# A decoder layer's gated FFN input projection as seven half-size products

## The chip, the cores and the metric

The kernel runs on one core of a Trainium2 chip. The metric is the device time of one launch, in microseconds, as the median of several runs. The profile is one further execution, taken with the hardware profiler; its span runs from the first instruction to the last.

## The reference, cut to what matters

One layer of a decoder: 512 tokens, 2048 features, float32 throughout. Two token mixers (a gated linear recurrence and a forgetting attention) are merged by gates, projected, normalised and added to the residual stream. Then comes a SwiGLU feed-forward part with 5632 inner features. Only its first product, 512 x 2048 by 2048 x 11264, is computed differently after the change.

```python
def rms_norm(x, w):
    y = x * lax.rsqrt(jnp.mean(x * x, axis=-1, keepdims=True) + RMS_EPS)
    return y * w

x = x + rms_norm(merged @ w_o, norm_mix_post)
h = rms_norm(x, norm_ffn_pre)
gate, up = jnp.split(h @ w_ffn_in, 2, axis=-1)     # D_FF = 5632 columns each
x = x + rms_norm((jax.nn.silu(gate) * up) @ w_ffn_down, norm_ffn_post)
```

## The kernel before, in words

TensorE (PE) multiplies in a float32 format whose operands are rounded (fp32r). Every float32 operand is therefore split into a high and a low part, and one product is three accumulating matmuls (`mm3`, L151 to L155, with the weights stationary; `mm3t`, L157 to L161, with the activations stationary).

All weights pass as one list `seq` of pieces of 128 x 1024 values. `make_w` (L125) loads a piece into one of three raw buffers on SP's queue, copies it to fp32r on ACT (`wh`, L137) and subtracts on DVE to get the rest (`wl`, L138). There are five buffers each of `wh` and `wl` (`NHALF`). `next_w` (L144) makes the wanted piece and the two that follow it in the list (`AHEAD` is 3) and hands out the wanted one.

The order of the work on each engine is not the order of the program text. A planner runs through the traced program with its own costs and places each instruction, earlier ones in the text first, as soon as its operands and a free buffer are there; what comes out is a fixed order for each engine and each queue. `tc.issue_after` and `tc.keep_in_program_order` add edges to it.

The stages: projections of the first norm's output and the mixers; gates and merge; the output projection w_o; FFN in; FFN down. `rows_product` computes w_o and FFN down in token rows, with eight banks of PSUM (four token tiles by two blocks of 512 columns) for each half of the 2048 columns. Of the second half the last four row tiles (`TAIL`) run token tile by token tile, so the four pieces of weights that they use stay in their buffers up to the end.

`wo_done` (L678 to L693) takes each block of the output projection: on DVE the product with the norm's gain, on ACT the square with its row sum, and, after the fourth block of a token tile, on POOL the power -0.5, on DVE four updates of the residual (L690), and their stores to DRAM (L691). After the second token tile `take_x1(0)` (L697) turns the first 256 tokens: PE transposes (L704), ACT multiplies by the gain of the next norm and rounds (L712), DVE forms the rest (L713). The other 256 tokens follow while the first two column pairs of FFN in are computed for 256 tokens at a time (tile f). The 1/rms of the token is taken from squares on ACT (L747) and multiplies the results afterwards, as a row along tokens (`r2b`).

The other 42 column pairs are two products of 48 matmuls each (tiles fg and fu): 128 weight columns stationary, 512 tokens moving. `swiglu` (L720) reads them from PSUM, on DVE with `r2b` (L723, L725), on ACT the sigmoid, on DVE two products more. Of the 44 results ten are stored in DRAM and read back for FFN down; the others stay in SBUF. `act_split` (L778) splits a result into its two parts for each half of FFN down.

Tiles of 128 x 512 values share two pools, 43 buffers named big and 32 named x.

Of the kernel before, what the change touches and what calls it, by code (L numbers as in the profile page):

```python
# [8 lines left out]
F32 = mybir.dt.float32  # L9
F32R = mybir.dt.float32r  # L10
# [17 lines left out]
NBIG = 43  # L28
# [3 lines left out]
AHEAD = 3  # L32
XAHEAD = 2
GATE_AHEAD = 5
NSPILL = 10
TAIL = 4
X1_AT = 6
# [3 lines left out]
def block_kernel(ctx: ExitStack, tc: tile.TileContext, x, w_in, b_fox_f, hgrn_lb_logits, hgrn_norm_w,  # L41
# [16 lines left out]

    psum = {}
# [18 lines left out]
    seq = []  # L78

    def cols(w, c0, kt):  # L80
        """one column tile of 128, as pieces of 8 row tiles"""
# [34 lines left out]
    korder = [(k + NSPILL) % KF for k in range(KF)]  # L116
    for half in range(2):
        for k in korder:
# [32 lines left out]
    def mm3(ps, wh, wl, xh, xl, first, last):  # L151
        """one accumulating float32 product in float32r parts: w lo x hi + w hi x lo + w hi x hi"""
# [4 lines left out]
    def mm3t(ps, wh, wl, xh, xl, first, last):  # L157
        """the same with x stationary"""
# [4 lines left out]
    def proj(name, xs, n_k, kind="acc"):  # L163
        """[128 columns, tokens] of the next weight columns"""
# [8 lines left out]
    def split(src, name, kind="big"):  # L173
        """float32 -> two float32r parts whose sum it is"""
# [16 lines left out]
    def rsqrt_mean(dst, ssq, n):  # L191
        """dst = (ssq / n + eps) ** -0.5"""
# [5 lines left out]
    # x by tiles of 128 features, all tokens  # L198
# [6 lines left out]
    # per-feature vectors, one row of 128 each, then transposed  # L205
# [19 lines left out]
    # the token's 1/rms multiplies the projections afterwards  # L225
# [39 lines left out]
    def token_row(r, name):  # L265
        """[token, tile] -> the same values along tokens, on every partition"""
# [5 lines left out]
        row = big(name)  # L272
# [14 lines left out]
    # lower bounds: row 0 of the cumulated softmax over the two rows of logits  # L287
# [16 lines left out]
    chunk0 = big("chunk0", shape=(P, 256))  # L304
# [3 lines left out]
    # lmask[p, level, which, block, l]: which pairs part at a level (see hgrn_head)  # L308
    lmask = [big("lmask0", shape=(P, 4, 2, 64)), big("lmask1", shape=(P, 3, 2, 64))]
# [10 lines left out]
    # Inside a head the chunks of 128 tokens lie as 0, 2, then 1, 3 with their tokens reversed, so that one matrix  # L320
    # of 128 x 128 holds, for two chunks, the scores of all pairs that part at a level.
# [9 lines left out]
    def by_parity(fn, out, *ins):  # L331
        """fn on the even chunks, then on the odd ones, from token order into the paired one"""
# [8 lines left out]
    def hgrn_in(h, part, ps, r):  # L341
        """what a head takes from one of its four projections"""
# [26 lines left out]
    def hgrn_head(h, r):  # L369
        """the rest of a head, in steps"""  # L370
# [24 lines left out]
        # scores within a chunk of 128: the diagonal, then pairs (s, t) by the level at which they part  # L395
# [22 lines left out]
        for li, L in enumerate(LEVELS):  # L418
# [7 lines left out]
            # keys, then queries; each by pair of chunks, then position with the chunk's place in the pair at level L  # L426
# [59 lines left out]
    def step():  # L486
        """the heads under way, each a step further"""
# [45 lines left out]
    cum = big("cum", shape=(H, S))  # L533
# [12 lines left out]
    def fox_head(h, r):  # L546
        """the attention of a head, in steps"""
# [130 lines left out]
    def wo_done(t, c, ps):  # L678
# [13 lines left out]
        if t == 1:  # L692
            take_x1(0)  # L693

    x1s = []

    def take_x1(th):  # L697
        hs = slice(th * 256, (th + 1) * 256)
        for k in range(0, KD, 2):
            pt = bank(f"x1p{th}_{k}", (P, 2, 2, P))  # L700
            for kk in range(2):
                for t in range(2):
                    c, q = (k + kk) // 4, (k + kk) % 4
                    nc.tensor.transpose(out=pt[:, kk, t, :], in_=xr[2 * th + t][c][:, q * P : (q + 1) * P],  # L704
# [131 lines left out]
```

## Time and profile before

| what | value |
|---|---|
| median of 3 runs | 2919.47 us (2918.87 to 2919.93) |
| span of the profiled execution | 2918.0 us |
| the three runs above the profiled span | 0.9 to 1.9 us, the median 1.5 us |
| PE busy | 2893.9 us (99%), 13346 matmuls |
| weight loads of PE (PEld) | 2404.1 us (82%) |
| DVE busy | 1213.9 us (42%) |
| ACT busy | 893.8 us (31%) |
| POOL busy | 36.5 us (1%) |
| moved between HBM and the core | 302 MB, 104 GB/s in the mean |

The profiled execution has no launch time around its span that the page shows: its own time is the span, and the runs lie 0.9 to 1.9 us above it. Busy times of matmuls overlap, so that a busy PE can still issue faster or slower; its rate is read from the starts of neighbouring matmuls. DVE, ACT and POOL take their instructions one after the other in the planned order, and the busy times of neighbours on DVE and ACT overlap by a little.

### The profile page before, as it was taken

What the parts mean: (1) busy time and instruction counts of PE and PEld (TensorE: products, weight loads), DVE (VectorE), ACT (ScalarE), POOL (GpSimd) and SP (SyncE); (2) the same over time, 40 slices, a digit from 0 to 9 for tenths busy, and PEclk for the clock granted to TensorE, in tenths of its full rate; (3) what the DMA queues carried; (4) which work ended last, traced back from release to release, by engine and by line L of the source; (5) the groups of instructions that cost most, each with busy time, mean ns of one, the idle gap of its engine ahead of it and who ended that gap; (6) DMA issues with size and microseconds to landing.
All of it is one profiled execution on the core that took longest, in us unless ns stands there. A gap on an engine that the chain in (4) does not pass through costs nothing.

```text
span 2918.0 us, 32478 instructions
## 1 busy us (share of the span) xinstructions
PE 2893.9 (99%) x13346; PEld 2404.1 (82%) x13346; DVE 1213.9 (42%) x1747; ACT 893.8 (31%) x1165; POOL 36.5 (1%) x72
## 2 busy tenths in 40 slices
PE   9999999999999999999999999999999999999998
PEld 7788888888888888888898888888888888888887
DVE  4776665333343433342373333333333334334333
ACT  4554544222232342232252222222222223323231
POOL 0100000000000000000000000000000000000000
PEclk9999999999999999999999999999999999999999
DMA  6323233333333333352363333333333334222342
GB/s 159 102 71 86 75 87 82 99 94 102 94 88 88 88 91 94 97 170 94 109 194 106 110 103 94 101 94 96 100 94 101 94 100 145 95 96 99 108 144 95
DMA packets 438967, 302.06 MB, mean 104 GB/s; under 512 B 11241, under 2 KB 410650, under 8 KB 438818
## 3 DMA queue, kind: packets, MB, share of 16 engines
q1 hardware_dynamic: 438818, 299.98, 35.2%
q8 instruction: 105, 1.72, 0.2%
q14 instruction: 44, 0.36, 0.0%
HBM read 288.91 MB, written 11.03 MB: 103 GB/s over the span
## 4 chain that ended last, share of the span: by engine, by line
PE 98%; ACT 1%; DVE 1%; issue 0%; DMA 0%; POOL 0%; SPq 0%; DVEq 0%; POOLq 0%; ACTq 0%
PE dn L159 5%; PE dn L161 5%; PE dn L160 5%; PE fg L154 5%; PE fu L154 5%; PE fg L155 5%; PE fu L155 5%; PE fu L153 5%; PE fg L153 5%; PE b L153 3%; PE b L154 3%; PE b L155 3%; PE p L153 3%; PE p L154 3%; PE p L155 3%; PE ga L155 2%
## 5 line engine op out<-in xcount | busy, mean ns | idle before, releaser
L137 ACT ACTIVATE wh<-wr 128x1024 fp32r<-128x1024 f32 (+1 forms) x518 | 544.5, 1052 | 1566.3 <-PE fg L154 358.3
L138 DVE TENSOR_TENSOR wl<-wr,wh 128x1024 fp32r<-128x1024 f32 (+1 forms) x518 | 629.8, 1216 | 716.1 <-ACT wh L137 715.9
L153 PE MATMUL fg<-x1l,wh 128*128 128x512 f32 x672 | 261.4, 389 | 0.0
L154 PE MATMUL fg<-x1h,wh 128*128 128x512 f32 x672 | 261.4, 389 | 0.0
L155 PE MATMUL fg<-x1h,wl 128*128 128x512 f32 x672 | 261.4, 389 | 0.0
L153 PE MATMUL fu<-x1l,wh 128*128 128x512 f32 x672 | 261.4, 389 | 0.0
L154 PE MATMUL fu<-x1h,wh 128*128 128x512 f32 x672 | 261.4, 389 | 0.0
L155 PE MATMUL fu<-x1h,wl 128*128 128x512 f32 x672 | 261.4, 389 | 0.0
L153 PEld LDWEIGHTS fu<-x1l,wh 128*128 128x128 f32 x672 | 126.2, 188 | 26.2
L153 PEld LDWEIGHTS fg<-x1l,wh 128*128 128x128 f32 x672 | 126.2, 188 | 26.2
L154 PEld LDWEIGHTS fu<-x1h,wh 128*128 128x128 f32 x672 | 126.2, 188 | 26.1
L154 PEld LDWEIGHTS fg<-x1h,wh 128*128 128x128 f32 x672 | 126.2, 188 | 26.1
L155 PEld LDWEIGHTS fu<-x1h,wl 128*128 128x128 f32 x672 | 126.2, 188 | 26.1
L155 PEld LDWEIGHTS fg<-x1h,wl 128*128 128x128 f32 x672 | 126.2, 188 | 26.1
L725 DVE TENSOR_TENSOR act<-fu,r2b 128x512 f32<-128x512 f32 x42 | 29.0, 692 | 138.6 <-PE fu L155 138.6
L723 DVE TENSOR_TENSOR g<-fg,r2b 128x512 f32<-128x512 f32 x42 | 29.0, 692 | 138.3 <-PE fg L155 138.3
L153 PE MATMUL f<-x1l,wh 128*128 128x256 f32 x128 | 36.7, 288 | 0.0
L154 PE MATMUL f<-x1h,wh 128*128 128x256 f32 x128 | 36.2, 284 | 0.0
L155 PE MATMUL f<-x1h,wl 128*128 128x256 f32 x128 | 36.2, 283 | 0.0
L515 DVE TENSOR_TENSOR sga<-ya,sga 128x512 f32<-128x512 f32 x16 | 11.1, 692 | 52.8 <-PE ya L155 52.8
L508 DVE TENSOR_TENSOR sga<-ga,rb 128x512 f32<-128x512 f32 x16 | 11.1, 692 | 51.9 <-PE ga L155 51.9
L727 DVE TENSOR_TENSOR act<-act,g 128x512 f32<-128x512 f32 (+1 forms) x46 | 30.7, 668 | 1.4
(1944 smaller groups left out, 5927.7 us busy)
## 6 DMA issues: line engine op xcount, KB each, us to landing
wr<-in_w_ffn_in_dram SPq DMA_DIRECT2D x168, 512.0 KB, 3.9
wr<-in_w_in_dram SPq DMA_DIRECT2D x166, 512.0 KB, 3.9
wr<-in_w_ffn_down_dram SPq DMA_DIRECT2D x88, 512.0 KB, 3.4
wr<-in_w_o_dram SPq DMA_DIRECT2D x32, 512.0 KB, 3.2
wr<-in_w_up_a_dram SPq DMA_DIRECT2D x16, 512.0 KB, 4.1
wr<-in_w_up_b_dram SPq DMA_DIRECT2D x16, 512.0 KB, 3.9
wr<-in_w_ffn_in_dram SPq DMA_DIRECT2D x32, 256.0 KB, 3.6
wr<-in_w_in_dram SPq DMA_DIRECT2D x32, 128.0 KB, 2.2
```

The costliest lines, as they stand in the source:

```text
L137: hi = nc.scalar.activation(wh[:, 0:width], raw[:, 0:width], AF.Copy)
L138: lo = nc.vector.tensor_tensor(wl[:, 0:width], raw[:, 0:width], wh[:, 0:width].bitcast(F32), ALU.subtract)
L153: nc.tensor.matmul(ps, lhsT=wh, rhs=xl, start=first, stop=False)
L154: nc.tensor.matmul(ps, lhsT=wh, rhs=xh, start=False, stop=False)
L155: nc.tensor.matmul(ps, lhsT=wl, rhs=xh, start=False, stop=last)
L159: nc.tensor.matmul(ps, lhsT=xl, rhs=wh, start=first, stop=False)
L160: nc.tensor.matmul(ps, lhsT=xh, rhs=wl, start=False, stop=False)
L161: nc.tensor.matmul(ps, lhsT=xh, rhs=wh, start=False, stop=last)
L508: nc.vector.tensor_tensor(sg_, psg_, rb, ALU.mult)
L723: nc.vector.tensor_tensor(g, psg, r, ALU.mult)
L725: nc.vector.tensor_tensor(a, psu, r, ALU.mult)
L727: nc.vector.tensor_tensor(a, a, g, ALU.mult)
```

## The change: what it does

The projection is computed by one level of Strassen's scheme in the form with seven products. Features (8 row tiles of 128 each half, `KH`), tokens (256 each half) and the gate and up columns are the halves. With a, b, c, d for the 1024 x 128 pieces of the weights (a: first features, gate; b: first features, up; c: second features, gate; d: second features, up), the products are of h11 with a, h12 with c, s4 with d, h22 with a combination of all, and s1, s2, s3 with b - a, a + (d - b) and d - b. The combinations of weights are made in place by DVE on the raw pieces, before the split. Each product is 24 matmuls of 256 tokens.

- The input is normalised in full before the projection: after each token tile's residual update `wo_done` squares it again, takes the power, and multiplies the token rows; `r2b` is gone. `take_h` replaces `take_x1` and makes the token and feature combinations on DVE.
- Phase one computes p1 and p2 of the first five column tiles (`NJ0`) from the first 256 tokens. Phase two computes their other five products, with the four pieces loaded again as needed. The other 39 column tiles run all seven products in a row.
- The pieces of w_ffn_in no longer pass through `seq`, whose w_ffn_down pieces now follow those of w_o. They have their own functions (`raw_w`, `load_to`, `parts_to`): loads nine products ahead, splits three ahead, in the same `wh` and `wl` buffers. Pieces b and d (c too in phase one) use three raw buffers of a new pool that takes the room of six tiles moved to `headp`; `NBIG` is 37.
- All 44 results go to DRAM, and FFN down reads each of them twice, three ahead.

```diff
-    for th in range(2):
-        for k in range(0, KD, 2):
-            r = w_ffn_in[k * P : (k + 2) * P, :]
-            seq.append([((0, 512), 2, r[:, 0:256]), ((512, 1024), 2, r[:, DFF : DFF + 256])])
-    for j in range(2, KF):
-        cols(w_ffn_in, j * P, KD)
-        cols(w_ffn_in, DFF + j * P, KD)
...
             nc.sync.dma_start(x1d[t * P : (t + 1) * P, c_ * S : (c_ + 1) * S], x1)
-        if t == 1:
-            take_x1(0)
+            nc.scalar.activation(mo[t, c_], x1, AF.Square, accum_out=s2_[:, t, c_ : c_ + 1])
+        s = smallp.tile([P, 1], F32, name="wos")
+        nc.vector.tensor_reduce(s, s2_[:, t, :], AX.X, ALU.add)
+        r = smallp.tile([P, 1], F32, name="wor")
+        rsqrt_mean(r, s, D)
+        for c_ in range(4):
+            nc.vector.tensor_scalar_mul(mo[t, c_], xr[t][c_], r)
+        if t % 2 == 1:
+            take_h(t // 2)
...
+    def parts_of(src, i, names, kind):
...
+        nc.scalar.activation(hi, src, AF.Copy)
+        nc.vector.tensor_tensor(lo, src, hi.bitcast(F32), ALU.subtract)
...
+    def take_h(th):
+        for i in range(KH):
...
+            raw = big(f"hr{th}_{i}")
+            for kk in range(2):
+                k = i + kk * KH
+                nc.scalar.activation(raw[:, kk * 256 : (kk + 1) * 256],
+                                     pt[:, kk, :, :].rearrange("p t n -> p (t n)"), AF.Copy,
+                                     scale=w_fpre_f[:, k : k + 1])
+            if th == 0:
+                hraw.append(raw)
+                parts_of(raw, i, ("h11", "h12"), "x")
+                continue
+            h1 = hraw[i]
+            h11, h12, h21, h22 = h1[:, 0:256], h1[:, 256:512], raw[:, 0:256], raw[:, 256:512]
+            s32 = big(f"hs{i}")
+            nc.vector.tensor_tensor(s32[:, 0:256], h11, h21, ALU.subtract)
+            nc.vector.tensor_tensor(h21, h21, h22, ALU.add)
+            parts_of(raw, i, ("s1", "h22"), "x")
+            nc.vector.tensor_tensor(s32[:, 256:512], h21, h11, ALU.subtract)
+            nc.vector.tensor_tensor(h12, h12, s32[:, 256:512], ALU.subtract)
+            parts_of(s32, i, ("s3", "s2"), "big")
+            parts_of(h12, i, ("s4",), "big")
...
+    work = [(j, p) for j in range(NJ0) for p in ("p1", "p2")]
+    work += [(j, p) for j in range(NJ0) for p in ("p3", "p7", "p5", "p6", "p4")]
+    work += [(j, p) for j in range(NJ0, KF) for p in ("p1", "p3", "p7", "p5", "p6", "p2", "p4")]
...
+    def parts_to(i):
...
+            if p == "p7":
+                nc.vector.tensor_tensor(d, d, b, ALU.subtract)
+            elif p == "p5":
+                nc.vector.tensor_tensor(b, b, a, ALU.subtract)
+            elif p == "p6":
+                nc.vector.tensor_tensor(a, a, d, ALU.add)
+            elif p == "p4":
+                nc.vector.tensor_tensor(c, a, c, ALU.subtract)
+            src = {"p1": a, "p2": c, "p3": d, "p7": d, "p5": b, "p6": a, "p4": c}[p]
+            wh = wp.tile([P, 1024], F32R, tag="wh", name=f"fh{n}", bufs=NHALF)
+            wl = wp.tile([P, 1024], F32R, tag="wl", name=f"fl{n}", bufs=NHALF)
+            nc.scalar.activation(wh, src, AF.Copy)
+            nc.vector.tensor_tensor(wl, src, wh.bitcast(F32), ALU.subtract)
...
+    for n, (j, p) in enumerate(work):
+        load_to(n + LOAD_AHEAD)
+        parts_to(n + AHEAD)
...
+        for i in range(KH):
+            cs = slice(i * P, (i + 1) * P)
+            xh, xl = hx[i][WITH[p]]
+            mm3(ps, wh[:, cs], wl[:, cs], xh, xl, i == 0, i == KH - 1)
...
+        if p == ("p2" if j >= NJ0 else "p6"):
+            t_ = tt[j] = big(f"t{j}")
+            g1 = gt[j][:, second_half]
+            nc.vector.tensor_tensor(t_[:, first_half], prod[j, "p6"], g1, ALU.add)
+            if j >= NJ0:
+                nc.vector.tensor_tensor(gt[j][:, first_half], prod[j, "p2"], g1, ALU.add)
+            nc.vector.tensor_tensor(t_[:, second_half], prod[j, "p7"], t_[:, first_half], ALU.add)
+            nc.vector.tensor_tensor(ut[j][:, second_half], prod[j, "p5"], t_[:, second_half], ALU.add)
+            nc.vector.tensor_tensor(ut[j][:, first_half], ut[j][:, first_half], t_[:, first_half], ALU.add)
+        if p == "p4":
+            g, u, t_ = gt.pop(j), ut.pop(j), tt.pop(j)
+            nc.vector.tensor_tensor(g[:, second_half], t_[:, second_half], prod[j, "p4"], ALU.subtract)
+            nc.scalar.activation(t_, g, AF.Sigmoid)
+            nc.vector.tensor_tensor(g, g, t_, ALU.mult)
+            nc.vector.tensor_tensor(g, g, u, ALU.mult)
+            nc.sync.dma_start(actd[j * P : (j + 1) * P, :], g)
...
+    def act_load(n):
+        if n < 2 * KF and n not in act:
+            act[n] = big(f"act{n}")
+            nc.sync.dma_start(act[n], actd[n % KF * P : (n % KF + 1) * P, :])
...
-        return split(act[k], f"as{half}_{k}", kind="x")
+        for n in range(3):
+            act_load(half * KF + k + n)
+        return split(act.pop(half * KF + k), f"as{half}_{k}", kind="x")
```

Two products of 256 tokens share one bank of PSUM. For the column tiles from the sixth on they pair as p1 and p3, p7 and p5, p6 and p2, and p4 alone; the reads shown and a few copies and adds left out above take them from there.

## Rows read from the trace of the kernel before

**Rows 1.** The page's chain of waits, by engine.

```profile
PE 98%; ACT 1%; DVE 1%; issue 0%; DMA 0%; POOL 0%; SPq 0%; DVEq 0%; POOLq 0%; ACTq 0%
```

**Rows 2.** Busy time by stretch (us, engines in the header's order).

```profile
core 0: us, PE busy (x) PEld busy (x) DVE busy (x) ACT busy (x) POOL busy (x), PEclk, DMA share, GB/s
...
1464.50:1480.00 15.50, 15.37 (x127) 14.98 (x126) 14.60 (x25) 14.54 (x35) 0.54 (x1) 1.00 0.78 245
...
1600.00:2400.00 800.00, 800.00 (x3531) 662.66 (x3530) 275.77 (x295) 175.22 (x184) 0.00 (x0) 1.00 0.34 99
...
2900.00:2918.00 18.00, 10.29 (x46) 8.19 (x44) 12.15 (x23) 2.89 (x10) 1.63 (x3) 0.87 0.48 179
```

**Rows 3.** Tiles fg and fu (512 wide): ns min/median/max, first and last start.

```profile
L153 PE MATMUL fg<-x1l,wh x672: 389/389/396, 1515.8 to 2418.2; 128*128 128x512 f32 x168
...
L155 PE MATMUL fu<-x1h,wl x672: 388/389/389, 1527.1 to 2429.5; 128*128 128x512 f32 x168
```

**Rows 4.** Timeline of PE, 256 wide: start, us; first and last of 36.

```profile
1509.78 0.28 PE L154 MATMUL f<-x1h,wh 128*128 128x256 f32 x1
...
1513.98 0.28 PE L153 MATMUL f<-x1l,wh 128*128 128x256 f32 x1
```

**Rows 5.** Tile f: one of its three groups of weight loads.

```profile
L153 PEld LDWEIGHTS f<-x1l,wh x128: 186/192/192, 1464.5 to 1515.3; 128*128 128x128 f32 x128
```

**Rows 6.** Timeline of PE: the projection's first matmul, and the down product's.

```profile
1464.67 0.28 PE L153 MATMUL f<-x1l,wh 128*128 128x256 f32 x1
...
2431.27 0.50 PE L159 MATMUL dn<-wh,as_10l 128*128 128x512 f32 x1 [1.38 <-DVE as_10l L178]
```

**Rows 7.** Timeline of PE: transposes of x1, the first of four such rows.

```profile
1476.41 1.47 PE L704 MATMUL x1p<-ident,xr 128*128 128x128 f32 x12
```

**Rows 8.** Timeline of DVE: neighbours of 1024, 512 and 256 columns.

```profile
1487.50 2.35 DVE L138 TENSOR_TENSOR wl<-wr,wh 128x1024 fp32r<-128x1024 f32 x2
1489.77 0.68 DVE L268 TENSOR_TENSOR r2bd<-ident,r4b 128x512 f32<-128x512 f32 x1
1490.37 1.21 DVE L138 TENSOR_TENSOR wl<-wr,wh 128x1024 fp32r<-128x1024 f32 x1
...
1497.30 0.42 DVE L725 TENSOR_TENSOR act<-f,r2b 128x256 f32<-128x256 f32 x1
1497.64 0.41 DVE L726 TENSOR_TENSOR g<-g,g_0s 128x256 f32<-128x256 f32 x1
```

**Rows 9.** Timeline of ACT: copies of 256 (four), 1024 and 512 columns.

```profile
1483.20 1.63 ACT L712 ACTIVATE x1h<-x1p,vec 128x256 fp32r<-128x256 f32 x4
1484.86 1.06 ACT L137 ACTIVATE wh<-wr 128x1024 fp32r<-128x1024 f32 x1
1485.83 1.19 ACT L712 ACTIVATE x1h<-x1p,vec 128x256 fp32r<-128x256 f32 x3
...
2431.23 0.61 ACT L177 ACTIVATE as_12h<-act 128x512 fp32r<-128x512 f32 x1
```

**Rows 10.** Waits, 1520 to 2430 us: total, times, longest.

```profile
ACT wh L137 <- PE fg L154: 358.3, 82, 4.4
DVE wl L138 <- ACT wh L137: 320.4, 126, 4.1
```

**Rows 11.** Timeline of ACT, POOL and DVE: one token tile of the output projection.

```profile
1448.79 0.63 ACT L747 ACTIVATE mo<-xr 128x512 f32<-128x512 f32 x1
...
1451.17 0.56 POOL L196 TENSOR_TENSOR wor<-rs_v,mhalf 128x1 f32<-128x1 f32 x1 [5.20 <-DVE rs_v L195]
...
1451.77 2.74 DVE L690 SCALAR_TENSOR_TENSOR xr<-mo,wor,xr 128x512 f32<-128x512 f32 x4 [0.68 <-POOL wor L196]
```

**Rows 12.** Groups by line and shape: a product with one value per row.

```profile
L576 DVE TENSOR_SCALAR b0p<-b0p,sm 128x512 f32<-128x512 f32 x1 | 0.5, 486 | 0.0
```

**Rows 13.** DMA issues, 1520 to 2430 us: count, KB each, us to landing.

```profile
wr<-in_w_ffn_in_dram SPq DMA_DIRECT2D x160, 512.0 KB, 3.9
...
actr<-actd SPq DMA_DIRECT2D x10, 256.0 KB, 7.1
```

More of the change, by code (lines that the diff above doesn't have):

```diff
@@ L27 @@
 LEVELS = (64, 32, 16, 8, 4, 2, 1)
-NBIG = 43
+NBIG = 37
+NHEAD = 6
+NRAWX = 3
+NJ0 = 5
 NX = 32
@@ L32 @@
 AHEAD = 3
+LOAD_AHEAD = 9
 XAHEAD = 2
 GATE_AHEAD = 5
-NSPILL = 10
 TAIL = 4
-X1_AT = 6
 @with_exitstack
@@ L57, in big @@
         return bigp.tile(list(shape), dtype, tag=kind, name=name, bufs=NX if kind == "x" else NBIG)
+    top = {}
+    top["ctx"] = ExitStack()
+    headp = top["ctx"].enter_context(tc.tile_pool(name="headp", bufs=1))
     psum = {}
@@ L271, in token_row @@
         nc.tensor.matmul(pr, lhsT=onesm, rhs=dg, start=True, stop=True)
-        row = big(name)
+        row = headp.tile([P, S], F32, name=name)
         nc.vector.tensor_copy(row, pr)
@@ L532, in block_kernel @@
     nc.vector.scalar_tensor_tensor(fb, fb, 0.0, fa, ALU.min, ALU.subtract)
-    cum = big("cum", shape=(H, S))
+    cum = headp.tile([H, S], F32, name="cum")
     nc.vector.memset(fa, 1.0)
@@ new lines, in wo_done @@
+        r = smallp.tile([P, 1], F32, name="wor")
[4 more added lines that the diff above has]
+            take_h(t // 2)
+    KH = KD // 2
+    hraw = []
+    hx = [dict() for _ in range(KH)]
+    def parts_of(src, i, names, kind):
+        w = src.shape[-1]
+        if w == S:
+            hi, lo = big(f"h{names[0]}{i}h", F32R, kind=kind), big(f"h{names[0]}{i}l", F32R, kind=kind)
+        else:
+            both = big(f"h{names[0]}{i}", F32R, kind=kind)
+            hi, lo = both[:, 0:w], both[:, w : 2 * w]
+        nc.scalar.activation(hi, src, AF.Copy)
+        nc.vector.tensor_tensor(lo, src, hi.bitcast(F32), ALU.subtract)
+        for n, name in enumerate(names):
+            hx[i][name] = (hi[:, n * 256 : (n + 1) * 256], lo[:, n * 256 : (n + 1) * 256])
@@ new lines, in block_kernel, with key_of, load_to @@
+    ORDER = {"p1": "a", "p2": "c", "p3": "d", "p7": "b", "p5": "a", "p6": "", "p4": "c"}
+    ahead = {"w": 0, "l": 0}
+    def key_of(i):
+        return (work[i][0], i < 2 * NJ0)
+    def load_to(i):
+        while ahead["l"] < min(i, len(work)):
+            n = ahead["l"]
+            for which in ORDER[work[n][1]]:
+                raw_w(key_of(n), "fi", work[n][0], which)
+            ahead["l"] += 1
+    wparts = {}
+    def parts_to(i):
+        while ahead["w"] < min(i, len(work)):
+            n = ahead["w"]
+            ahead["w"] += 1
+            j, p = work[n]
+            key = key_of(n)
+            load_to(n + 1)
+            a, b, c, d = (raws.get(key + (x,)) for x in "abcd")
+            if p == "p7":
[11 more added lines that the diff above has]
+            nc.vector.tensor_tensor(wl, src, wh.bitcast(F32), ALU.subtract)
+            wparts[n] = (wh, wl)
@@ L767, in block_kernel @@
     with tc.issue_after(loads[-1].ins):
         wfp = row_vector("wfp", norm_ffn_post, "x")
-        for j in range(NSPILL):
-            act[j] = big(f"actr{j}", kind="x")
-            nc.sync.dma_start(act[j], actd[j * P : (j + 1) * P, :])
+    act = {}
+    def act_load(n):
+        if n < 2 * KF and n not in act:
+            act[n] = big(f"act{n}")
+            nc.sync.dma_start(act[n], actd[n % KF * P : (n % KF + 1) * P, :])
     sst = const.tile([P, NT, 4], F32, name="sst")
@@ L774, in block_kernel @@
     x1r = {}
-    X1R_AT = [korder[i] for i in (20, 25, 30, 35)]
+    X1R_AT = [20, 25, 30, 35]
     def act_split(half, k):
@@ L804, in down_done @@
             nc.sync.dma_start(out[t * P : (t + 1) * P, c_ * S : (c_ + 1) * S], mw[t, c_])
-    rows_product(act_split, korder, "dn", down_done)
+    rows_product(act_split, list(range(KF)), "dn", down_done)
+    top["ctx"].close()
     psum["ctx"].close()
```

105 lines of the change are left out of this document (43 added, 62 removed).

## The prediction, made before the changed kernel was run

> **What bounds the kernel now.** I read the chain of waits first: TensorE holds 98% of it [rows 1], so only time taken off TensorE, or stalls put on it, can move the end. The stretches by stage say the same for the FFN input projection: between 1600 and 2400 us PE is busy all 800 us at clock 1.00, DVE 276 us, ACT 175 us [rows 2]. A busy PE says nothing of its rate, because the matmuls overlap (389 ns long), so I take the rate from start to start. The fg and fu matmuls, 512 columns wide, run from 1515.8 (first fg) to 2429.5 us (last fu) [rows 3]: 42 x 96 = 4032 matmuls, 4031 steps in 913.7 us, 226.7 ns each. Their 256-wide kin of the first two column pairs start at 1509.78 and, 35 steps on, at 1513.98 us [rows 4]: 120.0 ns. Both have the same stationary tile and the same three-matmul helper. So half the width costs 53% of the time: 13 ns per matmul are independent of width. The weight load lasts 0.19 us [rows 5], longer than 120 ns, and still lies beside the matmuls.
>
> The projection spans 1464.67 to 2431.27 us [rows 6], 966.6 us: 384 x 0.120 = 46.1, plus 4032 x 0.2267 = 913.9, plus 32 of x1's transposes at about 0.12 (12 in 1.47 us [rows 7]) = 3.8, plus the row of 1/rms (about 1), plus a wait of 1.4 for the first split of the down product [rows 6]. That is the sum, so almost nothing in it is a stall.
>
> **The change part by part.** *Matmuls.* 44 column tiles x 7 products x 8 feature tiles x 3 = 7392 matmuls of 256 columns: x 0.120 = 887.0 us, against 960.0. The operation count falls by 1/8 (120 us of 960), but the 13 ns are paid 2976 times more: 73 us remain. The row of 1/rms goes too, and with it 1 us; the wait of 1.4 us at the down product should go, since its first rows then lie in DRAM long before. Gain with TensorE always fed: 75 us.
>
> The Trainium skill's page "TensorE: Matmul & The Clock Gate", section "Back-to-back issue gap", gives N/2.4 + 2.5 ns at the full clock: 216 ns for 512 columns and 109 for 256. By it the projection would have 912 us of matmuls before and 807 after, a gain of 105, and the kernel would end 32 us below my forecast. The trace disagrees in both widths (226.7 and 120.0) and decides; that outcome gets no chance of its own.
>
> *What feeds them, column tiles 5 to 43.* One column tile is 168 matmuls, 20.16 us. DVE has 7 splits and 4 weight combinations of 128x1024: start to start 1.13 (two in 2.35, one lasts 1.22 [rows 8]) gives 12.4; 7 adds or copies of 256 columns at 0.34 = 2.4; two products of 512 at 0.60 = 1.2. Sum 16.0 us of 20.16, 79%, where fg and fu took 35%. ACT has 7 copies at 0.97 (1484.86 to 1485.83), two narrow ones at 0.39 and a sigmoid at 0.6: 8.2 us [rows 9]. Neither exceeds PE, so I cost them at nothing; the cover is 4.2 us per column tile, and if it is gone DVE sets the pace. The DVE order is FIFO. Queued behind a split that waits for its ACT copy are the PSUM adds and the next combination, and PE waits for that split two products later.
>
> How far ahead the splits run depends on buffers. There are five pairs of wh and wl, and the trace shows their limit: ACT's copies waited 358 us for fg's matmuls to release one, DVE 320 us for ACT's copies [rows 10]. After the change the stream that follows w_o in the list is w_ffn_down, and the last calls of next_w in the output projection make its first two pieces. Their pairs are held until the down product. Three remain: one under PE, one ready, one being made. From the release to the moment of need are two products, 2 x 2.88 = 5.76 us. Copy and split need 1.06 + 1.22 [rows 8, 9]; ahead of the split DVE may have the five adds behind p2 (1.7) and one combination (1.13): about 5.1. It fits, barely. I take 0.1 us per column tile, 4 us; the bounds are 0 and the rival below.
>
> *The way in.* Before, x1 is split straight from the transposes and PE barely stalls. Now each token tile, after its x1 (four updates, 2.74 us), has four more squares on ACT (0.63 each), a second power on POOL (0.56) [rows 11] and four scalings (0.49 each [rows 12]): some 4 us of chain, on DVE, ACT and POOL. All eight feature tiles' operands are then made by DVE: from x1 of the second token tile (1451.77 + 2.74 = 1454.5) to the last split of column tile 4 I count on DVE, with the pitches of that view [rows 8]: 12 scalings at 0.41 (duration less the 0.08 by which neighbours overlap) 4.9; eight updates 5.5; four products with wpost 2.4; h of the first token half 8 x 0.60 = 4.8; h, s1 to s4 of the second half 8 x (5 x 0.34 + 2 x 0.60) = 23.2; phase one (p1 and p2 of five column tiles) 10 x 1.13 + 5 x 0.34 = 13.0; phase two 5 x (9 x 1.13 + 6 x 0.34 + 1.2) = 67. Sum 120.8 us, ending at 1575 without idle time. PE needs for the same stretch 35 x 2.88 + 3.8 = 104.6 us after 1464.67, ending at 1569. So here DVE is the bound, by at least 6 us. At the share it has in the nearest busy stretch, 14.60 of 15.50 [rows 2], it ends at 1583, and the chain of scalings opens with some 4 us in which it has little: 1587, a loss of 18. I take 20; the bounds are 6 and 50 (each of phase two's 25 splits waiting 1.06 for its copy, and PE without operands for another 18 while the second half is made).
>
> *Transfers.* Loads: 5 x 2 + 5 x 4 + 39 x 4 = 186 of 512 KB, as many bytes as before (168 and 32 halves). They land in 3.9 us [rows 13]; six raw buffers and nine products of lookahead cover that: nothing. The stores of act rise from 10 to 44 and stand on SP's queue ahead of later weight loads; a late store delays loads that have a column tile of lead: nothing. The down product reads act from DRAM twice, 88 x 256 KB with 7.1 us to land [rows 13], three k ahead, where one k lasts 24 x 0.2267 = 5.4: nothing, bound 5. The six tiles moved to headp and NBIG 37 leave the early stages as they are: nothing, bound 3 either way.
>
> *Sum.* 887.0 + 3.8 + 20 + 4 + 0.5 = 915.3 against 966.6: 51.3 us less, span 2866.7. The median of the runs stands 1.5 above the profiled span of 2918.0: 2868 us.
>
> **The rivals.** *The way in is covered.* If the planner uses DVE's gaps so well that only its 6 us are lost, and no product waits later, the gain is 69 and more: 2844 to 2852. For it: in the trace the planner weaves transposes and splits into the tail of the output projection with hardly a gap on PE. Against: DVE is the bound there by count. Chance 0.12.
>
> *DVE's order sets the pace.* If each of the seven splits waits w behind its ACT copy, a column tile takes 16.0 + 7w, and PE starves as soon as w passes 0.59 us. With w near 0.8 the whole gain is spent (51 us over 39 column tiles is 1.3 each). With the full copy, 1.06, it is 23.4 us, 3.3 more than PE needs: 39 x 3.3 = 127, and some 14 more in phase two, about 3005 us, slower than before. For it: three pairs of buffers, and DVE's waits for the copy already seen [rows 10]. Against: those waits were of an engine with nothing else to do; in the crowded stretch DVE was busy 94% [rows 2], and the planner can place combinations in the gap. Chance 0.08 for a partial case (2890 to 2913), 0.04 for break-even, 0.14 for slower.
>
> *The clock.* It fell to 0.87 where PE worked 10.3 of 18 us at the end [rows 2]; a stall of that kind in the way in would add some us, inside the bound of 50.
>
> **How the numbers follow.** The forecast holds 0.62, its own range 2852 to 2890. Range for 8 in 10: 2847 (gain without any loss of feeding, 75 us, is 2844) to 2912, which leaves out the slower case, break-even and a little of the covered one. A difference under 0.2% (6 us) could not be told from none: faster 0.82, same 0.04, slower 0.14.
>
> **What would show it.** Matmuls of the products 120 ns apart, 20.2 us per column tile from the sixth on: the pitch right. Gaps of PE before phase two, DVE near full there, and column tile 4 done near 1587: the way in right. DVE at 75 to 80% after that and ACT copies released by PE: the steady state right. If instead PE's idle time before the products is ended by DVE's splits throughout, with DVE idle for ACT, the order sets the pace and the forecast is wrong. It is also wrong if 256-wide matmuls into one bank run at another pitch than 120 ns.

## The result, and the profile after

The changed kernel takes 2882.95 us (median of four runs, 2881.64 to 2884.19). Its ratio to the kernel before is 0.9877, 95% interval 0.9862 to 0.9891. The forecast was 2868 us, range 2847 to 2912: the gain is 36.5 us where 51.3 were forecast. A fourth run of the kernel before took 3001.97 us, 2.8% above the other three, and is left out as a slow one. The profiled spans, 2882.0 against 2918.0, are 36.0 apart, and the rest of this section accounts for these.

The chain of waits by engine, which answers to [rows 1], has PE at 96% (98 before) and DVE at 2% (1 before):

```profile
PE 96%; DVE 2%; ACT 1%; issue 1%; DMA 0%; POOL 0%; SPq 0%; DVEq 0%; POOLq 0%; ACTq 0%
```

Busy time by stretch, columns as in [rows 2]:

```profile
1464.90:1480.60 15.70, 0.33 (x2) 0.02 (x1) 13.21 (x25) 12.64 (x31) 1.64 (x3) 0.61 0.48 149
1487.00:1491.00 4.00, 4.00 (x20) 4.00 (x20) 2.46 (x7) 1.59 (x4) 0.00 (x0) 0.50 0.01 4
1492.00:1520.00 28.00, 28.00 (x235) 28.00 (x235) 26.14 (x47) 19.50 (x35) 0.00 (x0) 1.00 0.46 132
1520.00:1540.00 20.00, 16.15 (x97) 14.97 (x96) 16.38 (x27) 10.43 (x19) 0.00 (x0) 0.74 0.28 80
1700.00:2300.00 600.00, 600.00 (x5002) 600.00 (x5002) 494.99 (x598) 259.58 (x299) 0.00 (x0) 1.00 0.40 118
2388.00:2393.00 5.00, 0.00 (x1) 0.00 (x1) 2.97 (x5) 2.75 (x5) 0.00 (x0) 0.69 0.93 354
2393.00:2397.00 4.00, 4.00 (x10) 3.18 (x11) 2.95 (x5) 1.83 (x3) 0.00 (x0) 0.54 0.88 291
```

The row of 600 us is the steady part. It holds 5002 matmuls, one each 119.95 ns, with PE never idle. The two ends are what went wrong: PE is empty in the first row and in the last but one, and the mean granted clock in the rows that follow is 0.50 (the lower of its two levels, 1.2 GHz) and 0.54.

The timeline of PE (start, duration, and in brackets the idle time before it with what ended it) shows both ends; it answers to [rows 6]:

```profile
1480.67 1.94 PE L724 MATMUL hp<-ident,mo 128*128 128x128 f32 x8 [15.44 <-DVE mo L696]
1486.76 5.38 PE L724 MATMUL hp<-ident,mo 128*128 128x128 f32 x24 [4.14 <-DVE mo L696]
1491.79 0.53 PE L151 MATMUL f0p<-hh110l,fh 128*128 128x256 f32 x1
...
1525.72 0.38 PE L151 MATMUL f0p<-hs,fh 128*128 128x256 f32 x1 [1.69 <-DVE hs L714]
1527.19 0.58 PE L153 MATMUL f0p<-hs10h,fl 128*128 128x256 f32 x1 [0.85 <-DVE fl L810]
...
2387.66 0.28 PE L153 MATMUL f43p<-hs17h,fl 128*128 128x256 f32 x1
2393.00 0.79 PE L157 MATMUL dn<-wh,as_0l 128*128 128x512 f32 x1 [5.06 <-DVE as_0l L176]
```

The tile of column tile 5's products dates the end of the way in, 1601.5 us:

```profile
L151 PE MATMUL f5p<-hh110l,fh x2: 283/283/283, 1601.5 to 1615.9; 128*128 128x256 f32 x2
```

So the projection, from the end of w_o at 1464.9 to the first matmul of the down product at 2393.0, takes 928.1 us against 966.6. Of these, 136.6 are the way in (104.6 of PE's work, 32.0 lost), 786.4 are 39 column tiles of 20.16, and 5.1 are the wait. That saves 38.5. The down product starts at the lower clock and takes 2.3 longer (489.0 against 486.7), and the stages before end 0.2 later: 36.0.

Of the 32.0 us lost, 19.6 are PE's two waits ahead of the transposes (15.44 and 4.14), and 8.4 lie between 1520 and 1540, where 97 matmuls need 11.6 us at 0.120. Some 3 more are the transposes at the lower clock: the 32 of these two rows take about 7 us, where 3.8 were counted.

Where this loss begins is told by DVE's timeline:

```profile
1467.70 0.69 DVE L714 TENSOR_TENSOR hh115l<-hr,hh115h 128x512 fp32r<-128x512 f32 x1 [0.55 <-ACT hh115h L713]
1468.31 0.68 DVE L678 TENSOR_TENSOR mo<-wo,wpost 128x512 f32<-128x512 f32 x1
...
1472.05 1.22 DVE L810 TENSOR_TENSOR fl<-fia,fh 128x1024 fp32r<-128x1024 f32 x1
...
1480.04 1.68 DVE L696 TENSOR_SCALAR mo<-xr,wor 128x512 f32<-128x512 f32 x4 [0.66 <-POOL wor L194]
1486.21 1.68 DVE L696 TENSOR_SCALAR mo<-xr,wor 128x512 f32<-128x512 f32 x4 [0.72 <-POOL wor L194]
```

The operands of the first product are there when its split fl ends, at 1472.05 + 1.22 = 1473.3. PE starts it at 1491.79, 18.5 us later, because PE's queue has the transposes of the second token half ahead of it. These need token tiles 2 and 3, counted from 0, scaled (the two rows of L696). Their norms start late: the product with wpost that begins the chain of token tile 2 runs at 1468.31, behind the first half's splits in DVE's queue. Two queues of fixed order, each with something not yet needed in front.

At the other end stands SP's queue:

```profile
2380.04 2.71 SPq L129 DMA_DIRECT2D wr<-in_w_ffn_down_dram  x2
2382.81 1.88 SPq L657 DMA_DIRECT2D wfp<-in_norm_ffn_post_dram  x4
2384.74 3.21 SPq L866 DMA_DIRECT2D act<-actd  x5
```

The first rows of act are fetched at 2384.74, 3 us before PE has run out of products; that is too late for a transfer, a copy and a split.

### The profile page after: what moved, and what is told of

It reads as the page before. It is cut to its first block, busy times and chain, and to the rows that moved or that the text cites. A ratio compares the mean times of both kernels' runs of the same rounds, so it can differ in the third digit from the quotient of the medians.

```text
span 2882.0 us, 39661 instructions
## 1 busy us (share of the span) xinstructions
PE 2829.7 (98%) x16320; PEld 2495.4 (87%) x16320; DVE 1624.4 (56%) x2311; ACT 1079.1 (37%) x1406; POOL 35.0 (1%) x75
## 4 chain that ended last, share of the span: by engine, by line
PE 96%; DVE 2%; ACT 1%; issue 1%; DMA 0%; POOL 0%; SPq 0%; DVEq 0%; POOLq 0%; ACTq 0%
PE dn L157 6%; PE dn L158 6%; PE dn L159 5%; PE b L151 3%; PE b L153 3%; PE b L152 3%; PE p L151 3%; PE p L152 3%; PE p L153 3%; PE ga L153 2%; PE ga L152 2%; PE gb L151 2%; PE gb L153 2%; PE gb L152 2%; PE ga L151 2%; PE wo L157 2%
## 5 line engine op out<-in xcount | busy, mean ns | idle before, releaser
L136 DVE TENSOR_TENSOR wl<-wr,wh 128x1024 fp32r<-128x1024 f32 (+1 forms) x334 | 404.8, 1212 | 528.3 <-ACT wh L135 527.2
L135 ACT ACTIVATE wh<-wr 128x1024 fp32r<-128x1024 f32 (+1 forms) x334 | 349.8, 1048 | 925.9 <-PE dn L159 155.1
L810 DVE TENSOR_TENSOR fl<-fia,fh 128x1024 fp32r<-128x1024 f32 x88 | 107.7, 1224 | 79.3 <-ACT fh L809 79.3
L809 ACT ACTIVATE fh<-fid 128x1024 fp32r<-128x1024 f32 x88 | 93.4, 1062 | 112.4 <-DVE fid L799 33.1
L809 ACT ACTIVATE fh<-fic 128x1024 fp32r<-128x1024 f32 x88 | 93.4, 1062 | 111.1 <-DVE fic L805 102.7
L810 DVE TENSOR_TENSOR fl<-fic,fh 128x1024 fp32r<-128x1024 f32 x88 | 107.8, 1225 | 34.9 <-ACT fh L809 34.7
L809 ACT ACTIVATE fh<-fia 128x1024 fp32r<-128x1024 f32 x88 | 93.4, 1062 | 90.4 <-DVE fia L803 47.6
L810 DVE TENSOR_TENSOR fl<-fid,fh 128x1024 fp32r<-128x1024 f32 x88 | 107.1, 1217 | 3.5 <-ACT fh L809 3.5
L805 DVE TENSOR_TENSOR fic<-fia,fic 128x1024 f32<-128x1024 f32 x44 | 53.8, 1224 | 1.3
L799 DVE TENSOR_TENSOR fid<-fid,fib 128x1024 f32<-128x1024 f32 x44 | 53.7, 1220 | 0.1
L724 PEld LDWEIGHTS hp<-ident,mo 128*128 128x128 f32 x64 | 10.0, 183 | 24.3 <-issue 15.7
```

The costliest lines, as they stand in the source:

```text
L135: hi = nc.scalar.activation(wh[:, 0:width], raw[:, 0:width], AF.Copy)
L136: lo = nc.vector.tensor_tensor(wl[:, 0:width], raw[:, 0:width], wh[:, 0:width].bitcast(F32), ALU.subtract)
L799: nc.vector.tensor_tensor(d, d, b, ALU.subtract)
L805: nc.vector.tensor_tensor(c, a, c, ALU.subtract)
L809: nc.scalar.activation(wh, src, AF.Copy)
L810: nc.vector.tensor_tensor(wl, src, wh.bitcast(F32), ALU.subtract)
```

## The experiments

Times are medians; "after" is the changed kernel, 2882.95 us. Differences of a few us against it are read together with the traces, since the intervals of the ratios are some 4 us wide to either side.

**1. The loads of act ahead of the four loads of wfp.**

```diff
-    with tc.issue_after(loads[-1].ins):
-        wfp = row_vector("wfp", norm_ffn_post, "x")
...
+    for n in range(3):
+        act_load(n)
+    with tc.issue_after(loads[-1].ins):
+        wfp = row_vector("wfp", norm_ffn_post, "x")
```

> Only the order of traced loads at the start of the down product changes: the first three loads of act are traced ahead of the four rows of the last norm's gain, which wait on the same SP queue for buffers named x. Theory (a queue holds act back): the 5.1 us without matmuls before the down product and some 2 us at the lower granted clock behind it go, and the time falls by 6 to 8 us against the changed kernel, to about 2876. Rival (act comes late because the loads themselves take 7 us after the last products, or because buffers named big are short): the gap stays, less than 2 us change.

It took 2880.84 us (0.9868, 0.9854 to 0.9883): 2.1 less than after. The wait before the down product fell only from 5.06 to 3.74, as PE's timeline has it:

```profile
2389.56 0.80 PE L157 MATMUL dn<-wh,as_0l 128*128 128x512 f32 x1 [3.74 <-DVE as_0l L176]
```

SP's queue says why:

```profile
2377.92 2.71 SPq L129 DMA_DIRECT2D wr<-in_w_ffn_down_dram  x2
2380.69 0.90 SPq L657 DMA_DIRECT2D wfp<-in_norm_ffn_post_dram  x2
2381.64 1.46 SPq L864 DMA_DIRECT2D act<-actd  x3
```

Two of wfp's loads and two weight loads are still in front. The 1.88 us of wfp were a part. What holds the queue is the first of these weight loads, which goes out only when the last combination on DVE frees a raw buffer, at 2377.9 here and at 2380.0 in after. SP's waits from 2360 to 2400 have the same line in both (total, times, longest):

```profile
SPq L129 <- DVE fic L805: 7.8, 1, 7.8
```

The theory that wfp alone held act back fell. The 2.1 us aren't the junction's either: the way in ends 2.1 earlier in this trace (column tile 5 at 1599.4), the wait is 1.3 shorter, and the down product takes 0.9 longer.

**2. The second token half's operands built after the third product** (its transposes then stand behind it on PE).

```diff
-        if t % 2 == 1:
-            take_h(t // 2)
+        if t == 1:
+            take_h(0)
...
+        if n == 2:
+            take_h(1)
```

> Only the place in the program where the second token half is turned changes: after the third product of phase one instead of ahead of it. Theory A (PE's order): phase one's first matmul stood at 1491.8 us behind 32 transposes that waited for the last token tiles, though its operands were there from 1473.3; it now starts near 1474, and as phase one (28.8 us) covers the making of the second half, the time falls by 12 to 18 us. Theory B (DVE's work sets the end of the way in, as predicted): phase one starts as early, but phase two then waits for the second half's operands, which DVE finishes at 1534 as before; the time falls by less than 6 us.

It took 2878.48 us (0.9861, 0.9846 to 0.9876): 4.5 less. The first product does start 20.7 us earlier, and all but 3.8 of these are lost again by column tile 5. PE's timeline, at the start and later:

```profile
1471.07 0.58 PE L151 MATMUL f0p<-hh110l,fh 128*128 128x256 f32 x1 [6.15 <-ACT fh L809]
...
1473.38 0.41 PE L151 MATMUL f0p<-hh111l,fh 128*128 128x256 f32 x1
...
1477.43 0.41 PE L152 MATMUL f0p<-hh117h,fh 128*128 128x256 f32 x1
...
1478.79 0.28 PE L151 MATMUL f0p<-hh112l,fh 128*128 128x256 f32 x1
1478.91 0.28 PE L152 MATMUL f0p<-hh112h,fh 128*128 128x256 f32 x1
...
1525.73 0.58 PE L151 MATMUL f0p<-hs16l,fh 128*128 128x256 f32 x1 [1.77 <-DVE hs16l L714]
```

Column tile 5 starts at 1597.7, where after has 1601.5. PE now meets the second half's splits sooner, and waits for them in phase two until about 1530. Since the last token tile is scaled at 1488.95, even 2.7 us later than in after, an earlier first product alone is worth little. The gain lies in the range of theory B (less than 6 us): the order on PE alone was not the cause. Whether the second half comes late for its norms or for DVE's work, this run can't tell.

**3. The norms of all four token tiles before any splits of h.**

```diff
-        if t % 2 == 1:
-            take_h(t // 2)
+        if t == 3:
+            take_h(0)
+            take_h(1)
```

> Only the place where the first token half is turned changes: after all four token tiles of the output projection instead of after the second one, so that the last tiles' norms stand ahead of it on DVE and ACT. Theory C (DVE's and ACT's order): the products with the gain of token tile 2 waited from about 1457 to 1468.3 behind the first half's splits; now the last rows are normalised by about 1476 instead of 1488, the second half is made some 10 us earlier, and the time falls by 5 to 12 us. Theory B (the sum of DVE's work): the order of the two does not matter to the sum, less than 4 us either way.

It took 2873.3 us (0.984, 0.9824 to 0.9857): 9.65 less. DVE's timeline has the last scalings 11.8 us earlier than after:

```profile
1474.40 1.68 DVE L696 TENSOR_SCALAR mo<-xr,wor 128x512 f32<-128x512 f32 x4 [0.72 <-POOL wor L194]
```

The first product starts at 1479.98 (PE's timeline), column tile 5 at 1591.0, 10.5 earlier. DVE is busy 126.19 of the 136.5 us to that point, 92%, where after had 127.78 of 147.0, 87%:

```profile
1454.50:1591.00 136.50, 120.51 (x925) 117.03 (x924) 126.19 (x199) 81.61 (x144) 2.72 (x5) 0.92 0.51 151
```

The gain lies in the range of theory C. The work of DVE is the same; its queue has the longest chain first, and less of it is idle.

**4. All five pairs of wh and wl for the projection** (the first two pieces of w_ffn_down made when the down product begins).

```diff
+    n_ahead = len(seq)
...
-        if i in made or i >= len(seq):
+        if i in made or i >= len(seq) or (i >= n_ahead and not state.get("down")):
...
+    state["down"] = True
```

> The first two pieces of the down product are made only once the down product is traced, so that all five pairs of wh and wl serve the FFN input projection instead of three. Theory (three pairs are enough once the products run, since PE was busy throughout from 1560 us): column tiles 5 to 43 stay at 20.16 us; on the way in two more splits are made ahead, which is worth 0 to 4 us; in the whole within 4 us of the changed kernel. Rival (the pairs are short): 5 to 15 us less, all of it before 1600 us.

It took 2878.79 us (0.9862, 0.9847 to 0.9876): 4.2 less, just above the theory's range and below the rival's. All of it is in the way in: column tile 5 starts at 1596.7, and the steady part keeps its 5002 matmuls in 600 us. Where PE does not starve, the two pairs are worth nothing. In the way in DVE is busy 18.87 of the 20 us from 1520, where after has 16.38, so more of its work is done there.

**5. Experiment 3, and the first three loads of act put 14 products before the end.**

```diff
...
+        if n == len(work) - 14:
+            for i in range(3):
+                act_load(i)
...
```

> The third experiment (first half turned after all four token tiles), and the down product's first three act loads traced 14 products ahead of the end, so that they stand on SP's queue ahead of the weight pieces that wait for a raw buffer until 2380 us. Theory (act's loads stood behind a weight load that waits for its buffer, and moving the gain's rows alone could not help): the 5.3 us without matmuls before the down product and the half clock behind it go, 6 to 8 us less than the third experiment's 2873.3, about 2866. Rival (something else holds the first split, as ACT's order): less than 2 us.

It took 2866.27 us (0.9818, 0.9801 to 0.9834): 7.0 less than experiment 3. PE's timeline has no wait left at the junction, and no slow matmuls behind it:

```profile
2375.40 0.28 PE L153 MATMUL f43p<-hs17h,fl 128*128 128x256 f32 x1
2375.52 0.40 PE L157 MATMUL dn<-wh,as_0l 128*128 128x512 f32 x1
2375.75 0.40 PE L158 MATMUL dn<-wl,as_0h 128*128 128x512 f32 x1
```

So the junction cost some 7 us: the wait of 5.06 and some 2 at the lower clock. The two traces have 5.5 less from column tile 5 to the down product and 2.2 less in the down product.

**6. DVE's work cut.** The four sums and differences per feature tile that form s1 to s4 are left out (the plain halves of h are used in their place): 32 operations of 256 columns, 10.9 us.

```diff
-            nc.vector.tensor_tensor(s32[:, 0:256], h11, h21, ALU.subtract)
-            nc.vector.tensor_tensor(h21, h21, h22, ALU.add)
...
-            nc.vector.tensor_tensor(s32[:, 256:512], h21, h11, ALU.subtract)
-            nc.vector.tensor_tensor(h12, h12, s32[:, 256:512], ALU.subtract)
...
```

> From the changed kernel, DVE's four sums and differences of 256 columns for each of the eight feature tiles are left out (the products then take the plain halves; the output isn't the reference's). That is 32 x 0.34 = 10.9 us less on DVE on the way in, nothing else. Theory B (DVE's work after the second half is normalised sets the end of the way in): 7 to 11 us less than the changed kernel's 2882.9. Rival (the chain of norms and PE's order alone): less than 3 us.

It took 2884.25 us (0.9879, 0.9864 to 0.9894): nothing gained. By stretch, the stall has only changed its place (after: 28.00 and 16.15 us of PE):

```profile
1492.00:1520.00 28.00, 22.06 (x156) 21.56 (x155) 18.60 (x30) 20.44 (x43) 0.00 (x0) 0.86 0.27 76
1520.00:1540.00 20.00, 20.00 (x169) 20.00 (x169) 13.97 (x14) 8.30 (x12) 0.00 (x0) 1.00 0.54 154
```

A product of column tile 1 waits for a weight copy by ACT:

```profile
1507.23 0.58 PE L151 MATMUL f1p<-hh110l,fh 128*128 128x256 f32 x1 [5.52 <-ACT fh L804]
```

and ACT makes it only after the second half's copies, which now run without a gap, 2.06 us for each feature tile (ACT's timeline, the last of them):

```profile
1504.00 0.90 ACT L729 ACTIVATE hr<-hp,vec 128x256 f32<-128x256 f32 x2
...
1506.05 1.12 ACT L804 ACTIVATE fh<-fic 128x1024 fp32r<-128x1024 f32 x1
```

The theory that DVE's sum of work alone sets the way in of this kernel fell: ACT's queue took DVE's place, and the start at 1492.6 stayed. But the run is no clean price of DVE's work. In after, ACT's order has four weight copies between 1494.98 and 1504.7, among the second half's copies; without the sums the planner placed all the second half's copies first.

**7 and 8. DVE's cover in the steady part.** Two of a column tile's seven weight splits are done twice (2.3 us more), then all seven (7.9 us more).

```diff
-            nc.vector.tensor_tensor(wl, src, wh.bitcast(F32), ALU.subtract)
+            for _ in range(2 if j >= NJ0 and p in ('p1', 'p3') else 1):
+                nc.vector.tensor_tensor(wl, src, wh.bitcast(F32), ALU.subtract)
```

> From the changed kernel, for column tiles 5 to 43 DVE makes the splits of p1 and p3 twice, 2.3 us more DVE work per column tile, in the order of the products. Theory (PE sets the pace and DVE has 3.5 to 4.2 us to spare per column tile of 20.16 us): column tiles stay at 20.16 us, within 4 us of the changed kernel. Rival (DVE's order, with its waits for ACT's copies, is near its limit): the column tiles grow by 0.5 us or more, 20 us or more in the whole.

> As the run before, but all seven splits of column tiles 5 to 43 are made twice: 7.9 us more DVE work per column tile. Theory (the pace is the larger of PE's 20.16 us and DVE's sum): by the pitches counted beforehand (16.0) 23.9 us per column tile, +146 us; by the busy share read from the changed kernel (16.6) 24.5 us, +170 us; PE's gaps end with DVE. If DVE's waits for ACT come on top (up to 1.06 each), 27 us or more per column tile, +270 us.

With two it took 2920.29 us (1.0004, 0.9994 to 1.0013), 37 more than after; with all 3149.06 us (1.0786, 1.0764 to 1.0808), 266 more. The steady stretch with two doubled:

```profile
1700.00:2300.00 600.00, 580.00 (x4775) 574.32 (x4774) 534.57 (x628) 243.65 (x283) 0.00 (x0) 1.00 0.39 113
```

with all doubled:

```profile
1700.00:2300.00 600.00, 514.05 (x3731) 502.68 (x3729) 536.34 (x597) 189.53 (x223) 0.00 (x0) 0.89 0.30 88
```

4775 matmuls are 28.42 column tiles of 168, so 21.11 us each, and 3731 make 27.0. DVE is not full in either (89% in both). Per column tile it works 18.8 us and stands 2.3 with two doubled, 24.2 and 2.9 with all. Its waits are those for the weight copy. Of after, of 7 and of 8 (total, times, longest, in 600 us):

```profile
DVE fl L810 <- ACT fh L809: 85.2, 88, 1.2
```

```profile
DVE fl L811 <- ACT fh L809: 62.9, 86, 0.9
```

```profile
DVE fl L811 <- ACT fh L809: 63.1, 45, 1.8
```

That is 2.2 and 2.8 us per column tile, all that DVE stands. Work and these waits together make the pace in both. If the 2.2 hold for after too, it needs 16.6 of work (494.99 over 29.77 column tiles) and 2.2 of waits from DVE in 20.16 us: the cover is 1.3 us, not 4.2. Experiment 7 bears this out without the waits: of 2.3 us more work, 0.95 showed in the column tile, so 1.3 were covered.

**9. Experiments 5 and 4 together.** The diff is those of 3, 4 and 5.

> The three edits that helped, together: the first half turned after all four token tiles, act's first loads traced early, five pairs of wh and wl for the projection. If they act at different places (the norms' chain, SP's queue, the splits of the way in), their gains add: 9.6 + 7.0 + 4.2 us from the changed kernel's 2882.9, about 2862. If the five pairs only shortened the stall that the norms' order had already shortened, it stays at 2866.

It took 2862.05 us (0.9803, 0.9788 to 0.9817): 57.4 less than before, 20.9 less than after, so the three gains add. Column tile 5 starts at 1586.7, DVE is busy 126.30 of the 132.5 us to there (95%), and the down product starts with no wait:

```profile
1454.50:1587.00 132.50, 118.34 (x926) 115.75 (x925) 126.30 (x197) 80.27 (x143) 2.73 (x5) 0.94 0.49 146
```

```profile
2372.91 0.40 PE L158 MATMUL dn<-wh,as_0l 128*128 128x512 f32 x1
```

**10. Seven column tiles in phase one** (on top of 9), so that PE has more to do before it needs the second half.

```diff
-NJ0 = 5
+NJ0 = 7
```

> The run before with seven column tiles in phase one instead of five. Theory (phase two's start is fixed by the second half's making, some 45 us after its last scaling, and PE has only 28.8 us of phase one to cover it): 11.5 us more cover, the stall at the start of phase two goes, 4 to 8 us less than the run before. Rival (splits of weights, on the same DVE and ACT, are what the stall waits for; more of phase one brings more of them): within 2 us of it or slower.

It took 2861.33 us (0.9801, 0.9786 to 0.9815), the same as 9. Between 1492 and 1520 PE is now full (28.00 against 23.64), and between 1520 and 1540 it has 16.13 us against 20.00: the stall moves behind the longer phase one. With 95% of DVE taken, the way in looks bound by DVE in this order; a run with less DVE work in it was not made, so that is argued.

**11. The normalisation of the input left out:** squares, power and scalings go, and the transposes take the rows as they are (on after, not on 9).

```diff
-            nc.scalar.activation(mo[t, c_], x1, AF.Square, accum_out=s2_[:, t, c_ : c_ + 1])
...
-            nc.vector.tensor_scalar_mul(mo[t, c_], xr[t][c_], r)
```

> From the changed kernel, the input's normalisation ahead of the projection is left out (no second squares, power and scalings; the residual rows are turned as they are; the output isn't the reference's). It prices that part of the change. If the chain of norms sets the way in, phase two starts earlier by the chain's length, 4 us for each of the last token tiles: 6 to 10 us less than the changed kernel. If DVE's and ACT's order around it matter and not its own length, less than 4 us.

It took 2869.31 us (0.9829, 0.9813 to 0.9845): 13.6 less than after, more than the 6 to 10 expected of the chain. The first product starts at 1478.7, column tile 5 at 1586.5. The chain of the norms, with the place that it has in the queues, is worth some 14 us. That includes its work: DVE is busy 121.4 us from 1454.5 to there, 6.4 less than in after. Experiment 3 gained 9.65 by order alone; that these are a part of the 14 is likely, but the two were not run together.

**12. Experiment 7 with p2 as fourth product**, to part the two neighbours for which a combination, a copy and a split follow each other.

```diff
-    work += [(j, p) for j in range(NJ0, KF) for p in ("p1", "p3", "p7", "p5", "p6", "p2", "p4")]
+    work += [(j, p) for j in range(NJ0, KF) for p in ("p1", "p3", "p7", "p2", "p5", "p6", "p4")]
...
```

> The kernel with two splits made twice (2920.3 us), its products in another order for column tiles 5 to 43: p2 fourth instead of sixth, so that the split of c, c's combination and the split of that no longer stand one behind the other on DVE. Theory (DVE's 2.2 us of waits per column tile for ACT's copies, most of them in that chain, took the rest of its room): the waits fall to about 1.2 us, a column tile to 20.2 us, and the time by 30 us or more against 2920. Rival (DVE's work alone is too much): less than 10 us.

It took 2925.06 us (1.0019, 1.001 to 1.0028), 4.8 more than 7. The waits for copies remain, 58.3 us over 28.25 column tiles (2.1 each):

```profile
DVE fl L811 <- ACT fh L809: 58.3, 58, 1.4
```

They are fewer and longer; the order moved them and took none away. What makes the copies late can be read for one column tile of experiment 7, in which DVE waits 0.47, 0.87 and 0.84 us for these three (ACT's timeline):

```profile
1926.62 1.06 ACT L809 ACTIVATE fh<-fic 128x1024 fp32r<-128x1024 f32 x1 [0.63 <-PE f20p L152]
1930.31 1.06 ACT L809 ACTIVATE fh<-fic 128x1024 fp32r<-128x1024 f32 x1 [2.63 <-DVE fic L805]
1932.38 1.06 ACT L809 ACTIVATE fh<-fia 128x1024 fp32r<-128x1024 f32 x1 [1.01 <-PE f20p L152]
```

Two of the three copies, with 1.31 of the 2.18 us behind them, had waited for PE to release a pair of wh and wl; the middle one for a combination on DVE. So a rival to DVE's order stands untested: with five pairs instead of three (experiment 4's edit) the waits may be shorter and the cover larger. Experiment 7 was not run with them.

## Why the prediction came out as it did

**The matmuls: right.** 120.0 ns was read off 36 matmuls of 256 columns [rows 4]; 5002 of them gave 119.95. The term of 887.0 us and the 20.16 us for a column tile hold (786.4 us for 39). One gloss beside the sum does not add up: 120 us less 2976 times 13 ns would leave 80, not 73. An eighth of the 901 us without the 13 ns is 113, and that gives the 73 of the sum.

By the formula of the Trainium skill's page "TensorE: Matmul & The Clock Gate", section "Back-to-back issue gap", 256 columns take 109 ns, an estimate; the kernel after contradicts it with 119.95, as the kernel before did. The section gives this formula for a single matmul, and says that a stream of weight loads and matmuls departs from it; the prediction applied it to such a stream.

**The steady feeding: right in its cost, wrong in its cover.** It cost 0.2 us where 4 were taken, and DVE was at 82% against 79 counted. But "the cover is 4.2 us per column tile" was 20.16 less the work, as though DVE could be full. Experiments 7 and 8 show 1.3 with the three pairs that this kernel has. The prediction's own rival, DVE's order, has w = 2.2 / 7 = 0.31 us for each split in experiment 7, of the 0.59 at which PE starves: it didn't come true, but it was closer than "79%" sounds.

**The way in: the step that failed.** It was right that DVE's work is the heavier there, and 120.8 us counted stand against 127.78 busy, some of that for later column tiles. Wrong was "at the share it has in the nearest busy stretch", 94%: it had 87%, and column tile 4 ended at 1601.5, not 1587. In the new stage DVE has a chain of four token tiles, through ACT and POOL and back, queued behind splits for the first half. The prediction allowed "some 4 us" for this chain and placed it once, at the opening. Leaving the chain out gave 13.6 us (experiment 11), and putting it first 9.65 (experiment 3). Cutting 10.9 us of DVE's work, with the chain left where it stood, gave none (experiment 6), though ACT's order changed with it. With the order mended and five pairs (experiment 9), DVE has its 95% and column tile 4 ends at 1586.7, where the prediction had put it. The loss was 32.0 against the 20 taken: 12 of the 15.3 us by which the gain in the spans, 36.0, falls short.

**The junction: the second step that failed.** The wait of 1.4 us "should go, since its first rows then lie in DRAM long before". Rows in DRAM are not rows in SBUF: the loads were issued at 2384.74, behind a weight load that waited for a raw buffer. The prediction looked at later loads, three k ahead, which are in time (PE has no other wait in the down product), and not at the first, whose place in SP's queue no product gives a lead. The sum's 0.5, for which the prediction gives no row, may stand for what remains there; the wait took 5.1 and the lower clock about 2 more. Experiment 5 gave back 7.0 us.

**The balance.** Way in 12 short, junction 4.6 in the wait and 2.3 in the down product, steady feeding 3.8 better than taken: 12.0 + 4.6 + 2.3 - 3.8 = 15.1, against 51.3 - 36.0 = 15.3 in the spans; the stages before give the other 0.2. The time lies inside the range since the bound of the way in, 50 us, made the range wide. The sum itself missed by 15 of 51 us: 18.9 us of losses that it did not hold, less 3.8 of feeding priced too high. That the two offset each other in part is luck.

**The rivals.** That the way in is covered (2844 to 2852) was not seen, and no order tried here reached it: the fastest is 2861. That DVE's order sets the pace was not seen in the steady part. Stores and later loads cost nothing, as priced: PE has no wait in the steady part, and without the junction's wait the down product takes 487.1 us (experiment 9) against 486.7. The same goes for the tiles moved to headp: the output projection ends at 1464.9 against 1464.67 [rows 6]. The weight loads are 186 against 184, not "as many", which changes nothing.

## What to carry to other kernels

Price fewer but narrower matmuls by the rate of each width in the trace: here an eighth less arithmetic was 7.6% less time, 73 of the 960 us. Where a change moves the making of operands ahead of a stage, do not stop at the sum of each engine: walk each queue in its order, and ask at every entry of it what stands in front that is not yet needed; put the longest chain over several engines first. At a change of stages look at the first transfer by itself: it has no lead unless it is issued ahead of the loads that wait for buffers.

## What the runs showed of the hardware that was not expected

At the lower clock, 1.2 GHz, the matmul's time followed its width alone, in both widths seen. In experiment 2, at a granted 0.50 from 1472.9 to 1477.6, matmuls of 256 columns start 0.213 us apart (nineteen steps from 1473.38 to 1477.43), which is 256 columns at 1.2 GHz. Behind the junction of the changed kernel those of 512 start 0.426 apart, five steps in PE's timeline:

```profile
2394.02 0.63 PE L159 MATMUL dn<-wh,as_0h 128*128 128x512 f32 x1
...
2396.15 0.63 PE L158 MATMUL dn<-wl,as_0h 128*128 128x512 f32 x1
```

At 1.00 the narrow ones start 0.120 apart, 13 ns more than 256 columns at 2.4 GHz (106.7). So half the clock made them 1.78 times as long, not twice.

The clock had fallen where PE had stood, in the rows by stretch above: a mean of 0.61 in 15.7 us almost without work, 0.50 in the transposes behind them, and 0.54 behind the 5 us at the junction. In experiment 2 it is 1.00 again by 1478, in after by 1492. Where the junction had no wait, the first matmuls of the down product were at the full rate (0.23 us apart in experiment 5). So a wait of 5 us there cost 7.

An engine at 82% had no room for 2.3 us more in 20.16: DVE was busy 89% when the column tile grew, and stood the rest of it, 2.2 us per column tile, for copies by ACT.
